# A two-layer hybrid encoder: residual tiles in other buffers, and weight-splitting subtractions on GpSimd

## The chip, the cores and the metric

One core of a Trainium2 chip runs the kernel. The metric is the device time in microseconds (us) of one execution. The kernel before took 1229.7 us (median of 3 runs, 1227.62 to 1229.96).

## The reference

Two layers act on 512 tokens of width 1024, in float32. Each layer has a mixing half and an MLP half:

```
h = rmsnorm(x) @ w_in                       # split into parts for A, B and C
o_a = dilated biased attention   (6 heads)  # softmax(q k + bias) v
o_b = windowed biased attention  (4 query heads on 2 key heads, a sink logit)
o_c = latent attention, no bias  (6 heads, low-rank q and kv, rotary part)
mixed = concat(rmsnorm(o_a), rmsnorm(o_b), rmsnorm(o_c))
x = x + mixed @ w_out
x = x + relu(rmsnorm(x) @ w_up)^2 @ w_down
```

C is the "unbiased" attention, A and B are the biased ones.

## The kernel before, in words

**Number format.** Every matmul with float32 operands is made of products of a hi and a lo part. `split` (line 362) makes hi by a copy into the reduced format (ScalarE or VectorE, whichever the planner thinks is done first) and lo by a subtraction, source minus hi, on VectorE. `mm3` (line 403) adds three products: hi by hi, hi by lo, lo by hi. Weights go through `wload` (line 387): a DMA into one of two "raw" buffers, then `wsplit` (line 393) into one of four "whi" and four "wlo" buffers (NW, line 27).

**Order of the work.** The program text records operations; nothing is emitted until `Plan.schedule` (line 207) has put all of them in one order. It is a list scheduler: again and again it takes the operation that can start earliest by its estimated costs (`Plan.cost`, line 146), and among equals the one that stands first in the text. Buffers with one tag are handed out in the order of the text, apart from PSUM banks, which go in any order. Each engine, and the queue of DMA issues on SyncE, then runs its part of that order strictly in sequence. So text order sets priorities and buffer order, and an operation from further down fills gaps if its inputs and buffers are free.

**The mixing half** (`mix`, line 532). The input projections are cut into eight column groups, win0 and win(1) to win(7), of four 576-column or two 1024-column weight tiles each. The steps after the latent preparation are named in one string (line 911): w3 to w7 are input projections, C0 to C2 two heads each of the latent attention, A0 to A2 two heads each of the dilated attention, B0 and B1 two heads each of the windowed attention, gC and gA the group norms. Group B's norm follows (line 919). Then the residual x is loaded: `x_tiles` (line 341) puts three of its four 128-token blocks into the tile "v", which until then holds the values of attention A, and the fourth into a "ma" buffer, which attention A and B use for their bias rows (`master`, line 822). Line 925 issues the four loads. The output projection follows (lines 928 to 940), one group of w_out tiles after the other: C (3 tiles), A (3 tiles), B (2 tiles). For each half of the columns and each token block, a bank sums the products of the group, and VectorE adds the bank, scaled by the group's rstd, to the residual (line 936). After group B's add come the sums of squares and `norm_in` (line 447), the transposed input of the MLP.

The query and key tiles of attention C (`qc`, `kc`, line 644) are the two "tm9" buffers; the rotary and bias setup uses them before that (`setup`, line 463), with four loads and one store on GpSimd's queue.

**The MLP half** (`mlp`, line 956) works in four chunks. `pieces` (line 945) takes its hidden tiles from buffers that the mixing half no longer needs: "tm12", both "tm9" and one "ma" for the larger ones.

Of the kernel before, what the change touches and what calls it, by code (L numbers as in the profile page):

```python
# [10 lines left out]
F32 = mybir.dt.float32  # L11
F32R = mybir.dt.float32r
I32 = mybir.dt.int32
AF = mybir.ActivationFunctionType
OP = mybir.AluOpType
AX = mybir.AxisListType

D = 1024
# [3 lines left out]
NB = S // 128  # L22
# [3 lines left out]
FM = 16  # L26
NW = 4
QK = 4

G1, G2, GO, GQL, GKL, GQA, GKA, GQB, GKB, GQC, GKC, GQR, GKR, SNK, NPAR = (  # L30
    0, 8, 16, 24, 26, 27, 28, 29, 30, 31, 32, 33, 65, 97, 101)
# [90 lines left out]
class Plan:  # L122
# [23 lines left out]
    def cost(self, eng, method, out, ins):  # L146
        if method == "dma_start" and eng == "gpsimd":
            return 1000.0
        n = max([out.size() if isinstance(out, View) else 0] + [v.size() for v in ins if method == "tensor_reduce"])
        psum = any(v.buf.psum for v in ins) or (isinstance(out, View) and out.buf.psum)  # L150
        if eng == "tensor":
            if ins[0].dtype == F32R:
                return n / 2.4 + 12.5
            f = 2.0 if method == "transpose" else 4.0
            return f * max(n / 2.4, 54.0) + 2.0
        if eng == "vector":
            fast = method in ("tensor_scalar", "tensor_copy") and not psum and n > 64
            side = 60.0 if method in ("tensor_scalar", "scalar_tensor_tensor") and any(
                v.size() == 1 for v in ins[1:]) or method == "tensor_tensor_reduce" else 0.0
            return 70.0 + side + n / (1.92 if fast else 0.96) * (8.0 if method == "reciprocal" else 1.0)  # L160
        if eng == "scalar":
            return 93.0 * (len(ins) - 1) + (55.0 if psum else 95.0) + n / 1.2
        return 50.0 + n * 4 * 128 / 340.0

    def either(self, *calls):
# [5 lines left out]
    def record(self, eng, method, args, kw, alt=None):  # L171
# [6 lines left out]
        if alt:  # L178
            alt.alts[eng] = (method, args, kw, cost)
            return  # L180
        o = Op()
        o.i, o.alts = len(self.ops), {eng: (method, args, kw, cost)}
        o.after, o.need, o.bufs = set(), {self.gate} if self.gate else set(), []
        for views, write in ((ins, False), (outs, True)):
# [114 lines left out]
def kernel(  # L299
# [12 lines left out]
    pe, dve, act, dma, gps = (plan.engine(e) for e in ("tensor", "vector", "scalar", "sync", "gpsimd"))  # L312

    def T(shape, dtype, tag, bufs=1, pool="sb"):
        return plan.tile(pool, shape, dtype, tag, tag, bufs)

    def bank():
        return T([128, 512], F32, "bank", 8, "psum")

    def fmt(dt=F32R):  # L320
        return T([128, 512], dt, "fm", FM)

    def f32(a):
        return a.bitcast(F32)
# [14 lines left out]
    xs = T([S, D], F32, "xs", 1, "dram")  # L339

    def x_tiles():

        a, b = T([128, 3072], F32, "v", 1), T([128, 1024], F32, "ma", 2)
        return [a[:, i * D:(i + 1) * D] for i in range(3)] + [b[:, :D]]

    con_sb = T([128, 272], F32, "con_sb", 1)
    gps.dma_start(con_sb[:], con)
# [1 line left out]

    def P(l, i, n=1):  # L350
        return par_sb[:, l * NPAR + i:l * NPAR + i + n]


    def copy(out, src, scale=None):

        if scale is None:
            plan.either(("scalar", "activation", (out, src, AF.Copy), {}), ("vector", "tensor_copy", (out, src), {}))
        else:
            plan.either(("scalar", "activation", (out, src, AF.Copy), {"scale": scale}),
                        ("vector", "tensor_scalar", (out, src, scale, None, OP.mult), {}))  # L360

    def split(hi, lo, src, scale=None):

        copy(hi, src, scale)
        if scale is None:
            dve.tensor_tensor(lo, src, f32(hi), OP.subtract)
        else:
            dve.scalar_tensor_tensor(lo, src, scale, f32(hi), OP.mult, OP.subtract)
# [18 lines left out]
    def wload(src):  # L387
        n = src.shape[1]
        raw = T([128, 1024], F32, "raw", 2)[:, :n]
        dma.dma_start(raw, src)  # L390
        return wsplit(raw)

    def wsplit(raw):
        n = raw.a.shape[1]
        hi = T([128, 1024], F32R, "whi", NW)[:, :n]
        lo = T([128, 1024], F32R, "wlo", NW)[:, :n]
        split(hi, lo, raw)
        return hi, lo

    def at(w, c):  # L400
        return w[0][:, c], w[1][:, c]

    def mm3(out, a, b, start, stop):

        pe.matmul(out, a[0], b[0], start=start, stop=False, skip_group_check=True)
        pe.matmul(out, a[0], b[1], start=False, stop=False, skip_group_check=True)
        return pe.matmul(out, a[1], b[0], start=False, stop=stop, skip_group_check=True)
# [39 lines left out]
    def norm_in(k, gain):  # L447

        pt = bank()
        for b in range(NB):  # L450
            pe.transpose(pt[:, b * 128:(b + 1) * 128], x_t[b][:, k * 128:(k + 1) * 128], ident)
        hi, lo = fmt(), fmt()
        split(hi[:], lo[:], pt[:], gain)
        return hi, lo
# [77 lines left out]
    def mix(l, xg, st1):  # L532
# [48 lines left out]
        def qk4():  # L581
            g = T([128, 4, S], F32R, "qk", QK)
            return [g[:, i] for i in range(4)]
# [10 lines left out]
        vb = T([128, NB, 2, 3, 64], F32R, "vb", 1)  # L594
# [19 lines left out]
        for t in range(3):  # L614
# [3 lines left out]
            hi, lo = q4[2 * t:2 * t + 2]  # L618
# [224 lines left out]
        def group(os, first, mul, name):  # L843
            st = Stat(len(os), mul, name)
            for o in os:
                st.add(o)
            r = st.rstd()
            for i, o in enumerate(os):
                hi, lo = fmt(), fmt()
                split(hi[:], lo[:], o, P(l, GO + first + i))  # L850
                og[first + i] = (hi, lo)
            return r

        def ot(n):
            g = T([128, 3, S], F32, "o", 2)
            return [g[:, i] for i in range(n)]

        o_c, o_a = ot(3), ot(3)
# [35 lines left out]
        o_b = ot(2)  # L894
# [13 lines left out]
                       lambda qb: (max(0, qb - 1), min(NB - 1, qb + 1)), ls)  # L908
            normalise(o_b[pr], ls, rev)

        for step in "w3 C0 C1 C2 w4 w5 gC A0 A1 w6 A2 w7 gA B0 B1".split():
            if step == "gC":
                rc = group(o_c, 5, 1.0 / 384, "grc")
            elif step == "gA":
                ra = group(o_a, 0, 1.0 / 384, "gra")
            else:
                {"C": step_c, "w": step_w, "A": step_a, "B": step_b}[step[0]](int(step[1]))

        rb = group(o_b, 3, 1.0 / 256, "grb")


        nonlocal x_t
        x_t = x_tiles()
        for b in range(NB):
            dma.dma_start(x_t[b], (x if l == 0 else xs)[b * 128:(b + 1) * 128, :])
        st2 = Tokens("r2")
        xg2 = []
        for n, (ts, r) in enumerate((((5, 6, 7), rc), ((0, 1, 2), ra), ((3, 4), rb))):
            w = [wload(w_out[l, :, t * D:(t + 1) * D]) for t in ts]
            for h in range(2):  # L930
                hs = slice(h * 512, h * 512 + 512)
                for b in range(NB):
                    ps = bank()
                    for i, t in enumerate(ts):
                        mm3(ps[:], at(og[t], slice(b * 128, (b + 1) * 128)), at(w[i], hs), i == 0, i == len(ts) - 1)
                    dve.scalar_tensor_tensor(x_t[b][:, hs], ps[:], r[:, b:b + 1], x_t[b][:, hs], OP.mult, OP.add)
                    if n == 2:
                        st2.add(b, h)
                if n == 2:
                    xg2 += [norm_in(k, P(l, G2 + k)) for k in range(4 * h, 4 * h + 4)]  # L940
        return xg2, st2


# [1 line left out]
    def pieces():  # L945

        big, small = [], []
        for to, n, tag, w, bufs, k in ((big, 1024, "tm12", 3072, 1, 1), (big, 1024, "tm9", 2304, 2, 2),
                                       (big, 1024, "ma", 1024, 2, 1), (small, 768, "vb", 1536, 1, 1),
                                       (small, 768, "tm6", 1664, 1, 1), (small, 768, "o", 1536, 2, 2)):  # L950
            for _ in range(k):
                t = T([128, w], F32R, tag, bufs)
                to += [t[:, i * n:(i + 1) * n] for i in range(w // n)]
        return [(small[2 * j], small[2 * j + 1], big[2 * j], big[2 * j + 1]) for j in range(4)]

    def mlp(l, xg2, st2):
# [12 lines left out]
        for c in range(CH):  # L969
            quarter = []  # L970
            for q in range(4):
                t = T([128, 2048], F32, "qk", QK)
                dma.dma_start(t[:], w_down[l, :, (c * 4 + q) * 2048:(c * 4 + q + 1) * 2048])
# [83 lines left out]
    x_t = None  # L1057
    st1 = Stat(KT, 1.0 / D, "r1")
    xg = []
    for l in range(DEPTH):  # L1060
        xg2, st2 = mix(l, xg, st1)
        xg, st1 = mlp(l, xg2, st2)
    plan.emit()

# [90 lines left out]
```

## Time and profile before

| | before |
|---|---|
| median of 3 runs | 1229.7 us |
| profiled execution | 1230.45 us |
| its span, first to last instruction | 1228.7 us |
| mean granted TensorE clock | 0.993 |
| TensorE matmuls busy | 1203.5 us |
| VectorE busy | 1014.5 us |
| ScalarE busy | 629.0 us |
| GpSimd busy | 3.5 us |

The first layer's mixing half ends at about 273 us of the span; its MLP half reaches to about 631 us, where the second layer repeats the pattern. In the rows, PE is TensorE, PEld its weight loads, DVE VectorE, ACT ScalarE, POOL GpSimd, SP SyncE; "q" marks an engine's queue that issues DMAs. Nearly all operations carry line 295, where the planner emits them, so they are told apart by their tiles, written out<-in. Tiles "tm" are those of the tags tm6, tm9 and tm12. Matmul ends are modelled, so the distance of two starts tells more of TensorE's pace than a matmul's length.

### The profile page before, as it was taken

To read this page: it belongs to the slowest core of one execution; us is meant where nothing else is said; L and a number is where in the kernel's file an instruction comes from. 1 tells how busy PE (TensorE), PEld (TensorE's weight loads), DVE (VectorE), ACT (ScalarE), POOL (GpSimd) and SP (SyncE) were. 2 spreads that over 40 slices of the span, in tenths; PEclk is the share of its full clock that TensorE was granted. 3 is DMA by queue.
4 is the path that set the end of the run, shared out by engine and by line. 5 is a ranking of instruction groups with operands and counts; after the bars stand their busy time and mean duration, and the time that the engine had idled before them with its cause. 6 is when DMAs were issued, how large, how long until landed. Compare 5 with 4: busy or idle time off the path is not lost.

```text
span 1228.7 us, 17782 instructions
## 1 busy us (share of the span) xinstructions
PE 1203.5 (98%) x6624; PEld 1032.6 (84%) x6624; DVE 1014.5 (83%) x1907; ACT 629.0 (51%) x1232; POOL 3.5 (0%) x10
## 2 busy tenths in 40 slices
PE   9999999899999999999999999898999999999998
PEld 8998979788888888888899989786888888888886
DVE  7799879798796886977958996997978869779686
ACT  6658678455343333333546684965544334334342
POOL 1000000000000000000000000000000000000000
PEclk9999999899999999999999999998999999999999
DMA  6311254533133042140152114454331422422301
GB/s 197 125 52 53 50 147 132 150 137 121 68 122 118 35 173 102 71 135 20 53 166 72 50 52 102 136 146 136 131 117 38 165 79 79 155 71 103 103 1 69
DMA packets 36357, 123.89 MB, mean 101 GB/s; under 512 B 4700, under 2 KB 5852, under 8 KB 32176
## 3 DMA queue, kind: packets, MB, share of 16 engines
q1 hardware_dynamic: 36048, 122.41, 31.7%
q8 instruction: 52, 0.85, 0.3%
q0 software_dynamic: 224, 0.36, 0.1%
q14 instruction: 33, 0.27, 0.1%
HBM read 108.29 MB, written 4.24 MB: 92 GB/s over the span
## 4 chain that ended last, share of the span: by engine, by line
PE 85%; ACT 7%; DVE 4%; DMA 2%; issue 2%; SPq 0%; ACTq 0%; DVEq 0%
PE bank L295 85%; ACT p L295 3%; ACT pt L295 2%; DVE p L295 1%; DVE pt L295 1%; ACT pvt L295 1%; ACT sq L295 1%; DVE wlo L295 1%; DMA v<-in_xT_dram 0%; DMA qk<-qk 0%; DVE v L295 0%; ACT tm L295 0%; DMA v<-in_x_dram 0%; DVE o L295 0%; ACT fm L295 0%
## 5 line engine op out<-in xcount | busy, mean ns | idle before, releaser
L295 PE MATMUL bank<-fm,whi 128*128 128x512 f32 x1024 | 315.8, 390 | 0.0
L295 PE MATMUL bank<-whi,fm 128*128 128x256 f32 (+2 forms) x1280 | 288.2, 310 | 1.3 <-ACT whi L295 1.0
L295 PEld LDWEIGHTS bank<-fm,whi 128*128 128x128 f32 x1024 | 192.2, 188 | 39.9
L295 PEld LDWEIGHTS bank<-whi,fm 128*128 128x128 f32 x1280 | 211.5, 190 | 13.0 <-ACT whi L295 1.3
L295 ACT ACTIVATE whi<-raw 128x1024 fp32r<-128x1024 f32 (+2 forms) x110 | 112.3, 1023 | 209.0 <-PE bank L295 157.1
L295 DVE TENSOR_TENSOR wlo<-raw,whi 128x1024 fp32r<-128x1024 f32 (+2 forms) x122 | 142.4, 1169 | 79.3 <-ACT whi L295 78.9
L295 PE MATMUL bank<-fm,wlo 128*128 128x512 f32 x512 | 199.3, 390 | 0.0
L295 PE MATMUL bank<-wlo,fm 128*128 128x256 f32 (+2 forms) x640 | 197.3, 309 | 0.2 <-DVE wlo L295 0.2
L295 PE MATMUL bank<-whi,tm 128*128 128x512 f32 x544 | 177.2, 390 | 0.0
L295 PEld LDWEIGHTS bank<-wlo,fm 128*128 128x128 f32 x640 | 121.6, 190 | 6.4 <-DVE fm L295 0.9
L295 ACT ACTIVATE whi<-pt 128x1024 fp32r<-128x1024 f32 x64 | 68.0, 1063 | 109.6 <-PE bank L295 90.1
L295 PEld LDWEIGHTS bank<-whi,tm 128*128 128x128 f32 x544 | 102.1, 188 | 22.2
L295 PE MATMUL bank<-wlo,tm 128*128 128x512 f32 x304 | 118.7, 390 | 0.0
L295 PEld LDWEIGHTS bank<-fm,wlo 128*128 128x128 f32 x512 | 96.1, 188 | 19.9
L295 ACT ACTIVATE whi<-qk 128x1024 fp32r<-128x1024 f32 x48 | 50.9, 1059 | 100.7 <-PE bank L295 100.7
L295 PE MATMUL bank<-qk 96*128 96x512 f32 (+3 forms) x304 | 89.8, 401 | 5.6 <-issue 4.5
L295 DVE TENSOR_TENSOR wlo<-qk,whi 128x1024 fp32r<-128x1024 f32 x48 | 57.9, 1219 | 31.0 <-ACT whi L295 31.0
L295 DVE TENSOR_TENSOR pt<-bank,pt 128x512 fp32r<-128x512 f32 (+2 forms) x128 | 79.4, 633 | 4.1 <-ACT pt L295 2.3
L295 PE MATMUL bank<-con_sb,p 128*128 128x128 f32 x464 | 75.9, 285 | 5.8 <-DVE nm L295 1.7
L295 DVE TENSOR_TENSOR wlo<-pt,whi 128x1024 fp32r<-128x1024 f32 x64 | 77.9, 1217 | 1.2 <-ACT whi L295 1.2
L295 ACT ACTIVATE pt<-bank 128x512 fp32r<-128x512 f32 (+2 forms) x128 | 68.7, 555 | 3.3 <-PE bank L295 2.0
L295 ACT ACTIVATE p<-p,nm 128x512 f32<-128x512 f32 (+2 forms) x80 | 52.0, 651 | 33.6 <-DVE nm L295 33.5
(182 smaller groups left out, 1867.6 us busy)
## 6 DMA issues: line engine op xcount, KB each, us to landing
qk<-in_w_down_dram SPq DMA_DIRECT2D x32, 1024.0 KB, 4.6
raw<-in_w_up_dram SPq DMA_DIRECT2D x64, 512.0 KB, 3.3
raw<-in_w_in_dram SPq DMA_DIRECT2D x28, 512.0 KB, 3.4
qk<-qk SPq DMA_DIRECT2D x78, 128.0 KB, 2.4
raw<-in_w_out_dram SPq DMA_DIRECT2D x16, 512.0 KB, 3.8
ma<-brow SPq DMA_DIRECT2D x12, 448.0 KB, 4.0
raw<-in_w_in_dram SPq DMA_DIRECT2D x8, 288.0 KB, 3.6
v<-in_xT_dram SPq DMA_DIRECT2D x6, 256.0 KB, 6.2
```

What stands on the lines that cost most here:

```text
L295: getattr(getattr(nc, o.eng), o.name)(*[real(a) for a in o.args], **{k: real(v) for k, v in o.kw.items()})
```

## The change

The residual is loaded right after group C's norm (step x) into the two "tm9" buffers, two blocks in each. The output projections become steps of the order string: pC and pA stand before gB, pB last. In the mixing halves `wsplit` makes hi on ScalarE always and lo on GpSimd; the planner gets a cost for GpSimd. The MLP's larger hidden tiles come from "tm12", "v" and both "ma" buffers.

```diff
+ORDER = "w3 C0 C1 C2 w4 w5 gC x A0 A1 w6 A2 w7 gA B0 B1 pC pA gB pB"
...
+        if eng == "gpsimd":
+            return 100.0 + 2.3 * n
...
     def x_tiles():
-        a, b = T([128, 3072], F32, "v", 1), T([128, 1024], F32, "ma", 2)
-        return [a[:, i * D:(i + 1) * D] for i in range(3)] + [b[:, :D]]
+        return [t[:, i * D:(i + 1) * D] for t in (T([128, 2304], F32, "tm9", 2), T([128, 2304], F32, "tm9", 2)) for i in range(2)]
...
+    mixing = [False]
...
         lo = T([128, 1024], F32R, "wlo", NW)[:, :n]
-        split(hi, lo, raw)
+        if mixing[0]:
+            act.activation(hi, raw, AF.Copy)
+            gps.tensor_tensor(lo, raw, f32(hi), OP.subtract)
+        else:
+            split(hi, lo, raw)
         return hi, lo
...
-        for step in "w3 C0 C1 C2 w4 w5 gC A0 A1 w6 A2 w7 gA B0 B1".split():
...
-        rb = group(o_b, 3, 1.0 / 256, "grb")
...
-        x_t = x_tiles()
-        for b in range(NB):
-            dma.dma_start(x_t[b], (x if l == 0 else xs)[b * 128:(b + 1) * 128, :])
-        st2 = Tokens("r2")
-        xg2 = []
-        for n, (ts, r) in enumerate((((5, 6, 7), rc), ((0, 1, 2), ra), ((3, 4), rb))):
+        def project(ts, r, done):
             w = [wload(w_out[l, :, t * D:(t + 1) * D]) for t in ts]
...
-                    if n == 2:
+                    if done:
                         st2.add(b, h)
...
+        st2 = Tokens("r2")
+        xg2, r = [], {}
+        for step in ORDER.split():
+            n = int(step[1]) if step[1:].isdigit() else step[1:]
+            if step == "x":
+                x_t = x_tiles()
+                for b in range(NB):
+                    dma.dma_start(x_t[b], (x if l == 0 else xs)[b * 128:(b + 1) * 128, :])
+            elif step[0] == "g":
+                o, t, m = {"C": (o_c, 5, 384), "A": (o_a, 0, 384), "B": (o_b, 3, 256)}[n]
+                r[n] = group(o, t, 1.0 / m, "gr" + n.lower())
+            elif step[0] == "p":
+                project({"C": (5, 6, 7), "A": (0, 1, 2), "B": (3, 4)}[n], r[n], n == "B")
+            else:
+                {"C": step_c, "w": step_w, "A": step_a, "B": step_b}[step[0]](n)
...
-        for to, n, tag, w, bufs, k in ((big, 1024, "tm12", 3072, 1, 1), (big, 1024, "tm9", 2304, 2, 2),
-                                       (big, 1024, "ma", 1024, 2, 1), (small, 768, "vb", 1536, 1, 1),
+        for to, n, tag, w, bufs, k in ((big, 1024, "tm12", 3072, 1, 1), (big, 1024, "v", 3072, 1, 1),
+                                       (big, 1024, "ma", 1024, 2, 2), (small, 768, "vb", 1536, 1, 1),
...
+        mixing[0] = True
         xg2, st2 = mix(l, xg, st1)
+        mixing[0] = False
         xg, st1 = mlp(l, xg2, st2)
```

## Rows read from the trace of the kernel before

**Rows 1.** Engines of the page: busy us, share of the span, instructions
```profile
PE 1203.5 (98%) x6624; PEld 1032.6 (84%) x6624; DVE 1014.5 (83%) x1907; ACT 629.0 (51%) x1232; POOL 3.5 (0%) x10
```

**Rows 2.** Busy time by stage: us, PE PEld DVE ACT POOL, clock, DMA share, GB/s
```profile
75.00:125.00 50.00, 48.26 (x342) 43.16 (x341) 48.17 (x100) 41.87 (x95) 0.00 (x0) 1.00 0.14 43
125.00:150.00 25.00, 24.96 (x204) 24.46 (x204) 21.78 (x61) 15.76 (x37) 0.00 (x0) 1.00 0.13 32
150.00:212.00 62.00, 58.93 (x426) 52.68 (x425) 52.46 (x133) 47.92 (x116) 0.00 (x0) 1.00 0.54 141
229.80:247.90 18.10, 14.35 (x76) 11.18 (x75) 13.85 (x49) 13.24 (x45) 0.00 (x0) 0.81 0.26 94
247.90:273.00 25.10, 25.10 (x134) 20.60 (x134) 24.67 (x56) 14.74 (x38) 0.00 (x0) 1.00 0.48 168
836.20:854.30 18.10, 14.37 (x68) 11.12 (x67) 13.02 (x46) 12.52 (x42) 0.00 (x0) 0.72 0.27 93
```

**Rows 3.** Groups of TensorE in 229.8 to 247.9 us: busy us, mean ns
```profile
L295 PE MATMUL bank<-con_sb,p 128*128 128x128 f32 x25 | 6.0, 359 | 1.3 <-ACT p L295 0.7 <-DVE nm L295 0.6
L295 PE MATMUL bank<-pt,vb 128*128 128x256 f32 x16 | 4.1, 355 | 0.2 <-DVE pt L295 0.2
L295 PE MATMUL bank<-qk 128*128 128x384 f32 x12 | 4.0, 402 | 0.1
```

**Rows 4.** Timeline of TensorE where it is dense: start us, length us
```profile
286.06 0.60 PE L295 MATMUL bank<-con_sb,v 128*128 128x128 f32 x4
286.41 0.48 PE L295 MATMUL bank<-fm,wlo 128*128 128x512 f32 x1
...
294.68 0.39 PE L295 MATMUL bank<-fm,wlo 128*128 128x512 f32 x1
...
295.36 0.39 PE L295 MATMUL bank<-fm,wlo 128*128 128x512 f32 x1
```

**Rows 5.** Waits by engine: us in total, times, longest us
```profile
DVE v L295 <- DMA v<-xs: 4.2, 1, 4.2
```

**Rows 6.** Timeline of VectorE, 224 to 234 us
```profile
227.37 0.15 DVE L295 SCALAR_TENSOR_TENSOR gra<-rs_b,rs_y 128x4 f32<-128x4 f32 x1
231.08 1.41 DVE L295 SCALAR_TENSOR_TENSOR v<-bank,grc,v 128x512 f32<-128x512 f32 x2 [3.56 <-DMA v<-in_x_dram]
```

**Rows 7.** Timeline of the queue of DMA issues, first layer
```profile
38.45 77.23 SPq L295 DMA_DIRECT2D raw<-in_w_in_dram  x10
140.68 0.33 SPq L295 DMA_DIRECT2D raw<-in_w_out_dram  x1
...
247.02 0.33 SPq L295 DMA_DIRECT2D ma<-in_x_dram  x1
```

**Rows 8.** Timeline of TensorE, the last transposes of attention C's queries and keys
```profile
121.72 0.60 PE L295 MATMUL bank<-con_sb,tm 128*96 128x128 f32 x4
```

**Rows 9.** The tile in_x_dram: its loads, issue to landing
```profile
DMA to landing us min/median/max: 3.5/4.6/5.4
```

**Rows 10.** Timeline of TensorE, 256 to 266 us: the sums over group B's heads
```profile
264.88 1.05 PE L295 MATMUL bank<-one,ssum 128*128 128x1 f32 x8
```

**Rows 11.** Groups of the first mixing half, 0 to 273 us: busy us, mean ns
```profile
L295 DVE TENSOR_TENSOR wlo<-raw,whi 128x1024 fp32r<-128x1024 f32 x21 | 25.4, 1214 | 1.8 <-ACT whi L295 1.7
...
L295 ACT ACTIVATE whi<-raw 128x1024 fp32r<-128x1024 f32 x19 | 20.0, 1060 | 23.4 <-DMA raw<-in_w_in_dram 12.2 <-PE bank L295 11.1
...
L295 DVE CAST whi<-raw 128x1024 fp32r<-128x1024 f32 x4 | 2.7, 685 | 1.0 <-PE bank L295 1.0
```

**Rows 12.** Timelines of TensorE and GpSimd: start us, length us, idle before and its end
```profile
15.51 1.02 PE L295 MATMUL bank<-tm,tm 32*10 32x512 f32 x2
...
26.06 0.52 POOL L295 DMA_DIRECT2D brow<-tm  x1 [21.99 <-DVE rs_a L295]
```

**Rows 13.** Groups of VectorE, 0 to 273 us
```profile
L295 DVE TENSOR_TENSOR ssum<-ssum,sq 128x512 f32<-128x512 f32 x12 | 8.2, 684 | 0.0
```

More of the change, by code (lines that the diff above doesn't have):

```diff
@@ L909, in step_b @@
             normalise(o_b[pr], ls, rev)
-        for step in "w3 C0 C1 C2 w4 w5 gC A0 A1 w6 A2 w7 gA B0 B1".split():
[L912 to L917, printed above, removed]
-        rb = group(o_b, 3, 1.0 / 256, "grb")
-        nonlocal x_t
-        x_t = x_tiles()
-        for b in range(NB):
-            dma.dma_start(x_t[b], (x if l == 0 else xs)[b * 128:(b + 1) * 128, :])
-        st2 = Tokens("r2")
-        xg2 = []
-        for n, (ts, r) in enumerate((((5, 6, 7), rc), ((0, 1, 2), ra), ((3, 4), rb))):
+        def project(ts, r, done):
             w = [wload(w_out[l, :, t * D:(t + 1) * D]) for t in ts]
@@ L936, in mix @@
                     dve.scalar_tensor_tensor(x_t[b][:, hs], ps[:], r[:, b:b + 1], x_t[b][:, hs], OP.mult, OP.add)
-                    if n == 2:
+                    if done:
                         st2.add(b, h)
-                if n == 2:
-                    xg2 += [norm_in(k, P(l, G2 + k)) for k in range(4 * h, 4 * h + 4)]
+                if done:
+                    xg2.extend(norm_in(k, P(l, G2 + k)) for k in range(4 * h, 4 * h + 4))
+        nonlocal x_t
+        st2 = Tokens("r2")
[13 more added lines that the diff above has]
+                {"C": step_c, "w": step_w, "A": step_a, "B": step_b}[step[0]](n)
         return xg2, st2
```

## The prediction

> **What bounds the kernel now.** I read the page's engine table first [rows 1]: TensorE is busy for 98% of the span, so a faster VectorE is worth only what TensorE waits for it. The stage table [rows 2] shows where TensorE is not fed. In 75 to 125 us (latent attention) and 150 to 212 us (biased attention) it lacks 1.7 and 3.1 us, with VectorE busy for 48.2 of 50 and 52.5 of 62 us. GpSimd does nothing in any of these rows. The poor stretch is 229.8 to 247.9 us, with its repeat in the second layer at 836.2: TensorE shows 14.4 us busy out of 18.1, at a granted clock of 0.81 and 0.72, a mean over parts at 2.4 and parts at 1.2 GHz. Right after, 247.9 to 273, it is full again at clock 1.00.
>
> What work was in the poor stretch? The groups of TensorE there [rows 3] are transposes, scores and PV products of the grouped-query attention (step B) and nearly no projection. In dense stretches [rows 4] three 512-column matmuls start in 0.68 us (0.227 each) and four transposes in 0.35 us (0.088 each); by columns I estimate 0.17 for 384 and 0.114 for 256. So the stretch holds 25 x 0.088 + 16 x 0.114 + 12 x 0.17 = 6.1 us, and the other 23 of its 76 instructions, priced as 256 columns, 2.6: some 8.6 us of work in 18.1 us, **9.5 us lost**. The second layer's stretch has the same length, fewer instructions (68) and a lower clock, so it loses no less: 19 us for both.
>
> Why? The waits [rows 5] show VectorE held by the residual's loads for 4.2 us in the second layer, and its timeline in the first [rows 6] shows what that does: adds of projection C stand in front of step B's first score and hold VectorE from 227.4 to 231.1 us. The last load is issued only at 247.0 us [rows 7], because its buffer, "ma", still serves step B's biases. Until then that block's banks are not evicted, projection C's weight tiles stay held, and projection A, which has no other obstacle, can't start.
>
> **The change, part by part.**
>
> *Residual in "tm9" from step x.* The last transposes that read the query and key tiles there start at 121.7 us [rows 8]. The queue of DMA issues then has nothing between 115.7 (38.45 + 77.23) and 140.7 us [rows 7], and DMA is 13% busy in 125 to 150 [rows 2]. Four loads a layer, landing after 3.5 to 5.4 us [rows 9], fit there: I cost the moved issues at nothing. The cover is that gap; they go ahead of the w_out loads, the qk copies and the bias loads of 140 us and later, and if the planner set them among those, a copy could wait for one load, up to 5 us once a layer. They leave the stretch in which step B's own copies run.
>
> *Projections C and A inside step B.* Projection A alone is 8 banks x 9 matmuls x 0.227 = 16.3 us of work, more than the 9.5 us lost. What sets the end then is projection B, which needs group B, whose sum over heads comes at 264.9 us now [rows 10]. The work done up to 273 us, without the loss, would end near 263.5; step B's chain loses the wait of 3.6 us on VectorE but shares VectorE with A's adds (0.7 us each, as C's in rows 6). I leave 1 us a layer lost in front of projection B: 19 - 2 = **17.0 us gained**. The bounds are nothing (the chain slips by as much) and 19.
>
> *lo parts on GpSimd.* By the code there are 29 subtractions a layer: 22 of 1024 columns, 6 of 576, 1 of 768. VectorE spends 1.21 us on one of 1024 [rows 11], by columns some 0.7 and 0.9 on the others: 26.6 + 4.2 + 0.9, about 32 us a layer, go. No row shows GpSimd computing on a whole tile. From below I bound its price by VectorE's 1.21 us; from above by the pace at which weights are used: a 1024-column tile of the input projections feeds 48 matmuls of 256 columns, 48 x 0.114 = 5.5 us, and beyond that GpSimd would be the bound. I take twice VectorE's time, 2.4 us, nearer to the row. Throughput is then covered, and four buffers of each part let tiles be ready ahead. Where they aren't (the first tile, the changeover from projection C to A) lo comes 0.7 to 1.2 us later, partly hidden by the products of the hi parts: +1.5 us in all, between 0 and 5. The Trainium skill (GPSIMD Engine Reference, Performance versus the Vector engine) states 4497 ns for 2048 columns, by which I would estimate some 2.3 us; nothing in the sum hangs on that.
>
> What VectorE gets back is worth at most TensorE's idle time in the two attention stretches, 1.7 + 3.1 us a layer [rows 2]. With a tenth to a fifth of VectorE's work gone I take back 3 us of the 9.6, between 0 and 8.
>
> *hi parts on ScalarE alone.* VectorE made 4 of the wide ones in the first layer, at 0.69 us; ScalarE takes 1.06 us for one [rows 11]. Some 4 us more a layer, on an engine with 9 us free in the 25 of 125 to 150 us [rows 2]: nothing. Without that cover it would be those 4 us.
>
> *GpSimd's own queue.* The setup loads are issued by 4.1 us now (26.06 less an idle time of 21.99), ahead of TensorE's setup product at 15.5 us [rows 12]. Behind the first or second subtraction they go out 5 to 10 us later, and TensorE's queue, which is in order, waits for them: 0 to 5 us once; I take +1.5. Behind the store of the bias row, which waits for VectorE until 26.1 us, one or two subtractions could queue, and the products that read them; those tiles are asked for ahead: nothing.
>
> *MLP pieces in "v" and "ma", group B after A in the text.* "v" is last read by step A, "ma" by step B's biases, both before the MLP writes them; TensorE loses nothing in 247.9 to 273 now. The order of the groups in their buffers stays C, A, B. Nothing.
>
> Sum: -17.0 - 3 + 1.5 + 1.5 = -17.0 us. The profiled execution took 1230.45 us (its span 1228.7 and 1.75 around it), 0.75 above the median of 1229.7; so **1213.5 us**. A measurement of this kernel can tell some 0.2%, 2.5 us, from no change.
>
> **A rule that speaks against it.** In these rows GpSimd never computes beside VectorE, so none shows whether they hinder each other. The Trainium skill (SBUF — State Buffer, Who interferes with whom) says that a VectorE instruction with two SBUF inputs and a GpSimd instruction that reads SBUF exclude one another: the second waits for the end of the first. By it the 3 us of relief become none, 1216.5 us, and more where the wait falls into a chain; no run here shows it yet, and it stands below as a rival, priced from rows.
>
> **The rivals.**
> - *Exclusion (the slower side).* VectorE's sums of squares add two SBUF tiles [rows 13], and its normalising and rstd chains do the like; with 133 instructions in 62 us [rows 2], about five of all kinds fall into a subtraction of 2.4 us, so most subtractions would hold VectorE once, for half their length, 1.2 us. If half of the 58 fall into a chain that TensorE waits for, 29 x 1.2 = 35 us are lost: 1230.45 - 17 + 35 = 1248. It decides from 17 / 58 = 0.3 us per subtraction that reach TensorE. For it: VectorE's load in 75 to 125 us. Against: attention's own instructions read a bank and at most one SBUF tile, and TensorE has other work in most stretches.
> - *Step B stays the bound.* A's eight adds (8 x 0.7, near 6 us) delay its chain, so some of TensorE's idle time moves in front of projection B: 4 us a layer, gain 17 - 8 = 9, 1221.5. For it: VectorE and ScalarE each already work 13 to 14 of the 18 us in which TensorE starves [rows 2]. Against: 3.6 us of the chain go.
> - *Full relief.* VectorE's 32 us a layer free 8 us of the attention stretches' idle time and step B leaves nothing: 1230.45 - 19 - 8 + 1.5 = 1205. Against: the same load on ScalarE, 41.9 of 50 us [rows 2].
> - *It doesn't do what it says*: the planner issues the loads late again. Nothing reads "tm9" after 121.7 us, so I give it no chance of its own.
>
> **How the numbers follow.** Forecast 0.52 (its own range 1208 to 1220), step B as the bound 0.15, full relief 0.13, exclusion 0.20. Of the last I put 0.06 within 0.2% (gain and loss cancel) and 0.14 above. Faster 0.80, same 0.06, slower 0.14. The range runs from 1202, full relief with its other terms at their best, to 1230, where exclusion has eaten the gain; left out are some 0.15 above and a little below.
>
> **What would show it.** Right: the residual's loads issued at 120 to 140 us and no wait of VectorE for them; projection A's 512-column matmuls between 230 and 250 us, at clock 1.00; mixing halves some 8 us shorter each, MLP halves unchanged; GpSimd near 2.4 us a tile. Wrong: VectorE's two-input instructions held beside GpSimd, TensorE waiting for "wlo", a gap in front of projection B or behind the setup loads at 10 to 20 us.

## The result, and the profile after

The changed kernel took **1303.9 us** (median of 4 runs, 1300.77 to 1305.47) against 1229.8 for the kernel before on the same chip: a ratio of 1.060, 95% interval 1.0589 to 1.0615, 74 us slower. The forecast was 1213.5 within 1202 to 1230, so both the sign and the range were wrong. The profiled execution took 1304.59 us, its span 1302.8, at a mean granted clock of 0.971 (0.993 before). From these means I estimate that TensorE stood at 1.2 GHz, the lower of its two levels, for some 76 us, 17 before. The lower clock is part of the loss, and no run here separates it from the rest.

The engines on the page of the kernel after, beside [rows 1]:

```profile
PE 1234.9 (95%) x6624; PEld 1052.4 (81%) x6624; DVE 1032.2 (79%) x1861; ACT 631.1 (48%) x1220; POOL 137.7 (11%) x68
```

Some 64 us of subtractions left VectorE, and yet its busy time rose from 1014.5 to 1032.2 us. So its other instructions took some 82 us more, and no table of waits shows why. By stage (columns as in [rows 2]):

```profile
0.00:75.00 75.00, 60.95 (x408) 57.31 (x409) 52.24 (x137) 40.19 (x97) 29.17 (x23) 0.92 0.42 130
75.00:125.00 50.00, 43.76 (x252) 38.13 (x252) 47.72 (x127) 31.92 (x72) 14.89 (x4) 0.81 0.14 46
150.00:212.00 62.00, 57.33 (x435) 52.75 (x434) 42.07 (x105) 37.52 (x91) 14.43 (x6) 1.00 0.42 112
250.00:275.00 25.00, 20.16 (x90) 15.86 (x89) 16.03 (x59) 8.72 (x27) 0.00 (x0) 0.79 0.29 81
320.00:610.00 290.00, 290.00 (x1284) 238.86 (x1283) 231.72 (x284) 112.08 (x138) 0.00 (x0) 1.00 0.29 99
675.00:725.00 50.00, 43.91 (x335) 42.97 (x335) 33.61 (x88) 24.39 (x72) 16.85 (x8) 0.97 0.24 70
```

The MLP (320 to 610 us) is full as it was. The time went in the mixing halves. Much of it went before 125 us, in the first input projections (0 to 75 us: 408 matmuls started) and in the latent attention's preparation (75 to 125 us: 252 started, 342 before, at a mean granted clock of 0.81). The kernel before, from 0 to 75 us:

```profile
0.00:75.00 75.00, 71.67 (x529) 68.23 (x530) 60.54 (x201) 47.70 (x120) 3.53 (x10) 1.00 0.47 146
```

Step B's poor stretch is still there, now around 250 to 275 us, at 0.79.

What does a held instruction look like? VectorE's timeline of the kernel after, in the first layer (start us, length us):

```profile
63.87 0.18 DVE L298 SCALAR_TENSOR_TENSOR rs_a<-rs_i 128x16 f32<-128x16 f32 x1
64.08 2.38 DVE L298 TENSOR_TENSOR rs_b<-rs_a,rs_v 128x16 f32<-128x16 f32 x1
66.38 0.44 DVE L298 TENSOR_REDUCE ssq<-sq 128x3 f32<-128x288 f32 x1
```

and GpSimd's timeline of the same kernel, with one subtraction that starts 0.05 us before it and one later:

```profile
64.03 2.40 POOL L298 TENSOR_TENSOR wlo<-raw,whi 128x1024 fp32r<-128x1024 f32 x1 [13.11 <-ACT whi L298]
...
90.53 7.23 POOL L298 TENSOR_TENSOR wlo<-raw,whi 128x1024 fp32r<-128x1024 f32 x1 [2.74 <-ACT whi L298]
```

A multiplication of 16 columns, 0.17 us elsewhere, lasts 2.38 us and ends with GpSimd's instruction (64.03 + 2.40). At 90.53 it goes the other way round: VectorE runs normalising and rotary instructions back to back, and GpSimd's 2.4 us become 7.23. All rs_b instructions of the kernel before and then of the kernel after (groups by tile: ns min/median/max):

```profile
L295 DVE TENSOR_TENSOR rs_b<-rs_a,rs_v x78: 147/165/183, 25.0 to 904.4; 128x4 f32<-128x4 f32 x30, 128x16 f32<-128x16 f32 x24, 128x8 f32<-128x8 f32 x12, 128x24 f32<-128x24 f32 x12
```

```profile
L298 DVE TENSOR_TENSOR rs_b<-rs_a,rs_v x78: 142/166/2386, 30.5 to 977.5; 128x4 f32<-128x4 f32 x30, 128x16 f32<-128x16 f32 x24, 128x8 f32<-128x8 f32 x12, 128x24 f32<-128x24 f32 x12
```

The median has not moved; single instructions are 2.2 us longer. I summed these over the trace: an instruction of VectorE counts as held if it overlaps GpSimd's work on a tile and is over 0.1 us longer than the median of the same instruction in the kernel before (those without a counterpart there are left out). That gives 38 held instructions and 63 us, most of the 82. Of these, 22 instructions and 42 us belong to rstd chains (some ten small instructions each that make one over a root mean square; their tiles are rs_...). What TensorE sees of two of them, in the timelines of VectorE and then of TensorE:

```profile
47.93 1.25 DVE L298 SCALAR_TENSOR_TENSOR rs_y<-rs_b,rs_i 128x8 f32<-128x8 f32 x1
49.22 1.72 DVE L298 SCALAR_TENSOR_TENSOR rs_a<-rs_y 128x8 f32<-128x8 f32 x1
```

```profile
44.32 0.28 PE L298 MATMUL bank<-wlo,fm 128*128 128x256 f32 x1
52.40 0.90 PE L298 MATMUL bank<-con_sb,tm 128*128 128x128 f32 x3 [7.79 <-DVE tm L298]
```

Both belong to the rstd chain behind which "tm" is scaled. They add 2.6 us to that chain. The other 5 us of TensorE's wait are the rest of the chain and what stands in front of it. In the kernel before TensorE had work for that time (it is busy for 24.3 of the 25 us from 25 to 50 us), here it had none left. So what a hold costs also hangs on what covers its chain.

### The profile page after: what moved, and what is told of

Read it like the earlier page. It is cut to its first block, busy times and chain, and to the rows that moved or that the text cites. A ratio compares the mean times of both kernels' runs of the same rounds, so it can differ in the third digit from the quotient of the medians.

```text
span 1302.8 us, 17854 instructions
## 1 busy us (share of the span) xinstructions
PE 1234.9 (95%) x6624; PEld 1052.4 (81%) x6624; DVE 1032.2 (79%) x1861; ACT 631.1 (48%) x1220; POOL 137.7 (11%) x68
## 5 line engine op out<-in xcount | busy, mean ns | idle before, releaser
L298 PE MATMUL bank<-whi,fm 128*128 128x256 f32 (+2 forms) x1280 | 293.3, 317 | 5.8 <-ACT sq L298 4.9
L298 PEld LDWEIGHTS bank<-whi,fm 128*128 128x128 f32 x1280 | 218.4, 197 | 18.0 <-ACT sq L298 5.6
L298 POOL TENSOR_TENSOR wlo<-raw,whi 128x1024 fp32r<-128x1024 f32 (+2 forms) x58 | 134.2, 2317 | 811.4 <-ACT whi L298 806.5
L298 ACT ACTIVATE whi<-raw 128x1024 fp32r<-128x1024 f32 (+2 forms) x118 | 120.5, 1022 | 204.0 <-PE bank L298 122.5
L298 PE MATMUL bank<-wlo,fm 128*128 128x256 f32 (+2 forms) x640 | 203.5, 318 | 1.6 <-POOL wlo L298 1.6
L298 PEld LDWEIGHTS bank<-wlo,fm 128*128 128x128 f32 x640 | 126.2, 197 | 8.1 <-POOL wlo L298 2.1
L298 DVE TENSOR_TENSOR wlo<-raw,whi 128x1024 fp32r<-128x1024 f32 x64 | 81.3, 1271 | 64.1 <-ACT whi L298 63.8
L298 PE MATMUL bank<-whi,tm 128*128 128x512 f32 x288 | 98.5, 392 | 0.0
L298 PEld LDWEIGHTS bank<-con_sb,p 128*128 128x128 f32 x464 | 55.4, 148 | 21.5 <-ACT pt L298 4.6
L298 PE MATMUL bank<-con_sb,tm 128*128 128x128 f32 (+1 forms) x288 | 47.1, 305 | 26.2 <-DVE tm L298 25.4
```

The source lines that it names most:

```text
L298: getattr(getattr(nc, o.eng), o.name)(*[real(a) for a in o.args], **{k: real(v) for k, v in o.kw.items()})
```

## The experiments

Each run was timed in three rounds against the kernel before, which gave 1229.2 to 1229.7 us as the median beside them.

### The order alone, and GpSimd alone

The changed kernel with the weight tiles split as before:

```diff
-        if mixing[0]:
-            act.activation(hi, raw, AF.Copy)
-            gps.tensor_tensor(lo, raw, f32(hi), OP.subtract)
-        else:
-            split(hi, lo, raw)
+        split(hi, lo, raw)
```

> The changed kernel with hi and lo of the weight tiles made as before (lo on VectorE): the residual's buffers, the order of the projections and the MLP's buffers are left alone. Theory 1 (GpSimd's subtractions and VectorE's instructions hold each other): the whole loss of 74 us comes with the subtractions, so this kernel falls below the kernel before, 1215 to 1228 us; it does not reach 1213, since in the changed kernel the banks and weight buffers still kept projection A out of step B. Theory 2 (the new order costs the time: projections C and A take banks and VectorE from step B): 1245 us or more. Theory 3 (the loss is made in equal parts by both): near 1265.

Measured: 1235.3 us, ratio 1.0045 (1.0029 to 1.0062). This is none of the three theories' numbers: the order costs 6 us instead of gaining, and some 69 us come with the way the weight tiles are split, that is GpSimd's subtractions together with hi on ScalarE.

The kernel before with lo of the mixing halves alone on GpSimd (the flag and the planner's cost for GpSimd are as in the changed kernel):

```diff
-        split(hi, lo, raw)
+        if mixing[0]:
+            copy(hi, raw)
+            gps.tensor_tensor(lo, raw, f32(hi), OP.subtract)
+        else:
+            split(hi, lo, raw)
```

> The kernel before with only lo of the mixing halves' weight tiles on GpSimd; hi, the residual's buffers and the order string as before. Theory 1 (mutual holding): 1285 to 1310 us, with VectorE instructions of 16 or 24 columns that last 2 us and more beside a subtraction. Theory 2 (order): within 10 us of the kernel before.

Measured: 1294.9 us, ratio 1.0536 (1.0514 to 1.0559): GpSimd's subtractions cost 66 us in the old order too, with 35 held instructions and 55 us.

### Is it lo's lateness, or the holding?

Here VectorE makes lo as before, and GpSimd then works on the raw tile, which nobody reads any more. Two kernels in the same planned order differ in one instruction:

```diff
         split(hi, lo, raw)
+        if mixing[0]:
+            gps.tensor_tensor(raw, raw, f32(hi), OP.subtract)   # run 1
+            gps.memset(raw, 0.0)                                # run 2
```

> The kernel before, VectorE makes lo as before, and GpSimd makes the same subtraction a second time, into the raw tile that nobody reads any more. So lo is never late for a product; only raw is held longer. Theory 1 (holding): 30 to 70 us above the kernel before, since the price is VectorE's waiting and not lo's lateness. Theory 4 (lateness: GpSimd's 2.4 us in place of 1.2 us delay the products): within 10 us of the kernel before.

> As the run with the subtraction made twice, in the same planned order, but GpSimd fills the dead raw tile with zeros in place of the subtraction, so it reads nothing from SBUF. Theory 1 in the form that GpSimd's reading of SBUF is what excludes VectorE: within 8 us of the kernel before, small VectorE instructions beside a fill keep their 0.2 us. Theory 5 (any GpSimd instruction on SBUF holds VectorE, or the later release of raw costs the time): as far above the kernel before as the run with the subtraction, in proportion to GpSimd's busy time.

Measured: **1281.5 us** with the subtraction, ratio 1.042 (1.040 to 1.044), and **1232.7 us** with the fill, ratio 1.0029 (1.002 to 1.0039). GpSimd's groups and timeline, and VectorE's timeline, in the run with the subtraction:

```profile
L297 POOL TENSOR_TENSOR raw<-raw,whi 128x1024 f32<-128x1024 f32 x44 | 107.0, 2433 | 431.3 <-DVE wlo L297 264.4 <-issue 36.9 <-ACT pt L297 30.3
...
80.77 5.68 POOL L297 TENSOR_TENSOR raw<-raw,whi 128x1024 f32<-128x1024 f32 x2 [7.78 <-DVE rs_y L297]
...
81.69 2.42 DVE L297 SCALAR_TENSOR_TENSOR rs_a<-rs_y 128x24 f32<-128x24 f32 x1
84.03 0.21 DVE L297 TENSOR_TENSOR tbk<-sn,par_sb 128x64 f32<-128x64 f32 x1
84.17 2.33 DVE L297 TENSOR_TENSOR rs_b<-rs_a,rs_v 128x24 f32<-128x24 f32 x1
```

The same views in the run with the fill:

```profile
L297 POOL MEMSET raw<- 128x1024 f32 x44 | 42.5, 965 | 450.7 <-DVE wlo L297 292.0 <-ACT pt L297 26.7 <-DVE rqa L297 23.8
...
66.80 0.95 POOL L297 MEMSET raw<- 128x1024 f32 x1 [0.18 <-DVE rs_a L297]
...
66.71 0.21 DVE L297 TENSOR_TENSOR tbk<-sn,par_sb 128x64 f32<-128x64 f32 x1
66.84 0.17 DVE L297 TENSOR_TENSOR rs_b<-rs_a,rs_v 128x24 f32<-128x24 f32 x1
66.96 0.85 DVE L297 TENSOR_SCALAR tbk<-tbk 128x64 f32<-128x64 f32 x1
```

lo is made on VectorE in both, so GpSimd's lateness is no part of the 49 us between them. With the subtraction 31 instructions of VectorE are held for 50 us; the time is 52 us above the kernel before. With the fill, multiplications of two tiles run beside it at their usual 0.17 to 0.21 us; only a TENSOR_SCALAR waits for its end (66.96 + 0.85 is 67.81, the fill ends at 67.75).

The same count by kind of instruction tells which are held. Beside the subtraction they are 26 of 42 with two operands in SBUF and 5 of 9 TENSOR_SCALARs with one, but none of the 95 that read a bank and none of 22 TENSOR_REDUCEs. Beside the fill they are 6 of 7 TENSOR_SCALARs from SBUF and 3 of 59 instructions with two operands there.

Two other causes could lie in the 49 us. The raw buffer is free later behind the subtraction than behind the fill (2.4 us against 1.0). But by the tables of waits TensorE and its weight loads together wait for weight parts for 8.7 us with the subtraction and 3.2 with the fill, so at most 5.5 us lie there. And the mean granted clock is 0.979 against 0.994; the lower clock comes with the starving and is in the 49 us.

Does a hold last to the end of GpSimd's instruction? The next kernel cuts each repeated subtraction into four:

```diff
-            gps.tensor_tensor(raw, raw, f32(hi), OP.subtract)
+            for i in range(4):
+                q = slice(i * n // 4, (i + 1) * n // 4)
+                gps.tensor_tensor(raw[:, q], raw[:, q], f32(hi)[:, q], OP.subtract)
```

> As the run in which GpSimd repeats the subtraction into the dead raw tile (1281.5 us, 52 over the kernel before), but each repeat is cut into four instructions of a quarter of the columns; GpSimd's work and its operands are the same. Theory 1 in the form that an instruction is held until the other engine's current instruction ends: one hold lasts at most 0.6 us instead of 2.4, and the loss falls to 13 to 25 us, 1242 to 1255. Rival (the two engines share the bandwidth of one port, so that only the columns moved count): the loss stays near 52 us, 1275 to 1290.

Measured: 1271.3 us, ratio 1.034 (1.0324 to 1.0355). Timelines of GpSimd and VectorE:

```profile
83.48 4.32 POOL L297 TENSOR_TENSOR raw<-raw,whi 128x256 f32<-128x256 f32 x6
...
85.01 0.74 DVE L297 SCALAR_TENSOR_TENSOR rs_a<-rs_y 128x24 f32<-128x24 f32 x1
85.67 1.47 DVE L297 TENSOR_TENSOR rs_b<-rs_a,rs_v 128x24 f32<-128x24 f32 x2
87.06 0.78 DVE L297 SCALAR_TENSOR_TENSOR rs_y<-rs_b,rs_i 128x24 f32<-128x24 f32 x1
```

A single hold is now some 0.6 us, as a hold to the end of the instruction gives, but the saving I expected from it did not come: a chain meets the next quarter with its next instruction, so 76 instructions are held instead of 31, for 34 us in place of 50. The loss fell from 52 to 42 us only. GpSimd, for its part, is busy for longer (183 us in place of 130).

### Where on the path do the holds cost most?

The first kernel splits the tiles of w_in's groups 0 to 2, w_uq and w_ukv as before and uses GpSimd from step w3 on (the flag is set ahead of the order's loop):

```diff
+        mixing[0] = True
         for step in ORDER.split():
```

> The changed kernel (1304 us) with hi and lo as before up to step w3 (input column groups 0 to 2, w_uq, w_ukv: lo on VectorE), and on GpSimd from w3 on. Theory 1 (holding, dear where VectorE runs chains of small instructions on SBUF tiles: rstd, rotary parts, sums of squares): the first 75 us of each layer win back most of what they lost, 1255 to 1275 us, the rest stays with w3 to w5 beside the rotary part. Rival (late lo or the setup loads behind the subtractions at the start are the main price): the setup alone is once, under 5 us, so 1300.

Measured: 1286.2 us, ratio 1.046 (1.0445 to 1.0476), 18 us less than the changed kernel and not the 30 to 50 expected. Its first 50 us are as before (TensorE busy for 46.6), but the first subtraction now starts at 53.5 us and meets the rstd and rotary chains all the same; 28 instructions stay held for 49 us.

The second uses GpSimd for w_out's eight tiles a layer alone, in the better order of the next section:

```diff
+            mixing[0] = True
             w = [wload(w_out[l, :, t * D:(t + 1) * D]) for t in ts]
+            mixing[0] = False
```

> The kernel with the new order and the held scores, and of the weight tiles only w_out's eight a layer with hi on ScalarE and lo on GpSimd. There VectorE mostly reads banks, which GpSimd's subtraction did not hold. Theory 1 with that reading: within 4 us of the same kernel without GpSimd, either way. Relief theory (VectorE is short of time in step B): 3 to 8 us faster than it. Holding in all places: 29 of 58 holds, 10 us or more slower.

Measured: 1223.6 us, ratio 0.9953 (0.9938 to 0.9968), 12 us slower than the same kernel without it (1211.6), and not within 4 us as expected. Only 10 instructions are held, for 12.2 us, although the attention beside it mostly reads banks. That the two numbers agree is in part chance: TensorE also waits for "wlo" for 3.1 us in this run, and hi is on ScalarE. One of the ten, with one operand, in the timelines of GpSimd and then of VectorE:

```profile
215.04 2.41 POOL L298 TENSOR_TENSOR wlo<-raw,whi 128x1024 fp32r<-128x1024 f32 x1 [15.30 <-ACT whi L298]
```

```profile
215.47 2.01 DVE L298 TENSOR_SCALAR rs_v<-ssqa 128x16 f32<-128x16 f32 x1
```

### Why did step B stay starved?

In the run with the order alone the residual is loaded long before and VectorE waits for no load, yet TensorE is busy for 14.7 us of 20.2 only, at a granted clock of 0.75 (stage table of that run):

```profile
232.40:252.60 20.20, 14.71 (x71) 11.31 (x71) 15.18 (x50) 14.86 (x47) 0.00 (x0) 0.75 0.49 147
```

In the changed kernel's timeline of TensorE, step B's scores come in bursts of eight matmuls, two to a bank:

```profile
262.48 1.34 PE L298 MATMUL bank<-qk 128*128 128x256 f32 x8
263.66 0.40 PE L298 MATMUL bank<-wlo,fm 128*128 128x512 f32 x1
263.90 0.39 PE L298 MATMUL bank<-whi,fm 128*128 128x512 f32 x1
264.13 1.53 PE L298 MATMUL bank<-qk 128*128 128x256 f32 x8
```

These two bursts take eight banks, as many as the kernel has. Scores need only the query and key tiles and stand ahead of the projections in the text, so the planner can give them every bank that comes free. Projection C's seventh add comes at 264.3 us, its eighth at 289.8, and until then its three weight tiles stay held. The test is to let the planner set a score of step B only behind the eviction of the second score before it:

```diff
+                    if ahead and len(seen) >= ahead:      # 2 in step B, 0 elsewhere
+                        plan.gate = seen[-ahead]
                     score(qb, sc, j0, nk)
+                    plan.gate = None
...
+                    if ahead:
+                        seen.append(<the eviction just recorded>)
```

> The kernel with the new order and lo on VectorE (1235 us), and one thing more: in the planner's order a score of step B may stand only behind the eviction of the second score before it; nothing else changes. Theory 6 (step B's scores run ahead, each takes a bank, and so the planner places projection A behind step B): projection A's 512-column matmuls now lie between step B's, the two poor stretches of some 9.5 us go, 1210 to 1222 us. Rival 7 (step B's own chain on ScalarE and VectorE sets the end, or the weight splits that stand in front of its softmax there): no change within 5 us, or slower, as scores come later.

Measured, with lo on VectorE: **1211.6 us**, ratio 0.9859 (0.9842 to 0.9875), below both kernels. TensorE's groups in 225 to 250 us, first of the run with the order alone, then of this one, with this one's stage:

```profile
L298 PE MATMUL bank<-whi,fm 128*128 128x512 f32 x15 | 4.9, 391 | 0.0
```

```profile
225.00:250.00 25.00, 25.00 (x151) 21.73 (x150) 22.99 (x68) 17.81 (x57) 0.00 (x0) 1.00 0.53 154
...
L298 PE MATMUL bank<-whi,fm 128*128 128x512 f32 x41 | 14.2, 402 | 0.0
```

The projections now lie between step B's instructions, 41 of their hi matmuls in place of 15, and the clock stays at 1.00. Did the residual's place matter at all? The same hold in the kernel before:

> The kernel before with the held scores alone: a score of step B may be planned only behind the eviction of the second score before it. The residual is still loaded at the end into the tiles of attention A and a bias buffer. The prediction's cause (the residual's late loads hold VectorE and projection C's banks, so A can't start): the poor stretch stays, 1225 us or more. Theory 6 (the scores take the banks, whatever the residual does): the poor stretch goes here too, 1211 to 1220 us; the move of the residual is then worth the difference to the run with both, 1211.6.

Measured: 1215.2 us, ratio 0.9885 (0.987 to 0.9899). Its stage and its queue of DMA issues:

```profile
225.00:250.00 25.00, 23.85 (x143) 20.06 (x142) 22.67 (x72) 18.27 (x56) 0.00 (x0) 1.00 0.65 177
...
246.19 0.33 SPq L295 DMA_DIRECT2D ma<-in_x_dram  x1
```

The last block is issued at 246.2 us, as late as in [rows 7], and the poor stretch is gone all the same. So the scores that run ahead were the cause; that they do it through the banks is argued from the bursts above. The new order (the residual, the projections and the MLP's buffers together) is worth 3.6 us beside the hold (1215.2 to 1211.6), which is hardly clear of the noise, since the intervals of the two ratios just overlap. Without the hold it cost 6.

### The other parts, in the order with held scores

> The changed kernel (1304 us) with the held scores alone. If the banks of step B and the holding by GpSimd are two costs that add, it gains the 24 us that the same hold gave with lo on VectorE: 1275 to 1285 us. If GpSimd's holding sets step B's pace anyway, 1295 or more.

> The new order with held scores, lo on VectorE, and hi of the mixing halves' weight tiles on ScalarE always, as in the changed kernel. The prediction's term (ScalarE has the time, nothing): within 3 us of 1211.6. Rival (hi stands in ScalarE's queue ahead of attention's exponentials and waits there for a weight buffer): 4 us a layer, near 1219.

> As the run with hi on ScalarE always, but the lo parts of the mixing halves' weight tiles are left out: GpSimd fills them with zeros behind hi, which held VectorE for 4 us in all in the run with fills, and VectorE loses 32 us of work a layer. The planner is given the fill's measured 0.9 us. What it tells is what VectorE's relief is worth without the holding. The prediction's term: 3 us faster than with lo on VectorE (0 to 8), 1204 to 1212. Rival 8 (with VectorE relieved the planner sets the input projections earlier, and TensorE has nothing left beside the latent attention's normalising chain): slower than it, 1215 to 1225.

The edits are the hold in the changed kernel, and, in place of GpSimd's subtraction there, one on VectorE (`dve.tensor_tensor`), or a fill that leaves lo out (`gps.memset(f32(lo), 0.0)`, planned behind hi). Each row changes one thing more:

| kernel | us | ratio (interval) | step |
|---|---|---|---|
| new order, held scores | 1211.6 | 0.9859 (0.9842 to 0.9875) | |
| hi on ScalarE always | 1215.8 | 0.9889 (0.9874 to 0.9903) | +4.2 |
| lo a fill on GpSimd: VectorE relieved | 1225.3 | 0.9964 (0.9951 to 0.9977) | +9.5 |
| lo subtracted on GpSimd | 1281.4 | 1.0423 (1.0406 to 1.0441) | +56.1 |
| scores not held: the changed kernel | 1303.9 | 1.0602 (1.0589 to 1.0615) | +22.5 |

The first step is hardly clear of the noise either (the two intervals touch). Rows 2 and 4 differ by one edit, lo on VectorE or on GpSimd: 65.6 us, with 38 held instructions and 63 us of holds.

The third row surprises. The stages of the run with hi on ScalarE, and then of the run with the fill:

```profile
60.00:80.00 20.00, 20.00 (x166) 20.00 (x166) 20.00 (x74) 10.44 (x23) 0.00 (x0) 1.00 0.26 80
80.00:100.00 20.00, 19.13 (x134) 17.03 (x133) 18.65 (x46) 16.98 (x38) 0.00 (x0) 1.00 0.10 27
```

```profile
60.00:80.00 20.00, 18.06 (x134) 15.87 (x132) 20.00 (x78) 13.48 (x27) 1.91 (x2) 1.00 0.36 106
80.00:100.00 20.00, 18.78 (x111) 15.88 (x112) 18.87 (x45) 16.82 (x41) 0.00 (x0) 0.91 0.00 1
```

In 60 to 100 us TensorE starts 245 matmuls instead of 300, while VectorE, busy for nearly all of it in both, works on the latent attention's normalising chain. What is missing there are products with weight tiles. TensorE's matmuls that read "whi" (us, busy, clock, DMA share, GB/s), in the run with hi on ScalarE and then in the run with the fill:

```profile
60.00:100.00 40.00, 25.53 (x133) 1.00 0.18 53
...
120.00:140.00 20.00, 4.07 (x20) 1.00 0.13 48
```

```profile
60.00:100.00 40.00, 10.23 (x57) 0.96 0.18 54
...
120.00:140.00 20.00, 15.22 (x80) 1.00 0.13 31
```

Up to 60 us the second run is ahead by only 14 of them (249 to 235); most of what covered the chain now comes after it. So the planner set the cover elsewhere. This run also gives the planner a shorter time for GpSimd, so the 9.5 us are the relief together with another plan, and which of the two moved the projections stays open. The step of 56.1 us takes in lo's lateness; the pair of runs with lo on VectorE puts the holding at 49.

## Why the prediction was wrong

**The larger failed step: lo on GpSimd, put at +1.5 us of lateness and -3 us of relief.** The sum had no term for VectorE's instructions being held; the holding stood beside it as a rival at 0.20. The runs showed some 69 us for the split on GpSimd and ScalarE (1235.3 to 1303.9), most of it holding: 49 us by the pair of runs with lo on VectorE. That is about three quarters of the 90 us between forecast and measurement; the order is the rest.

**The other failed step: "projection A, which has no other obstacle, can't start".** It took the residual's wait of 3.6 us on VectorE for the cause of the 9.5 us lost. It was no more than a symptom: with the residual as late as before and the scores held, TensorE is busy for 23.85 us of 25 at a clock of 1.00. The obstacle was step B's scores, planned ahead, with the banks that they take and projection C's weight tiles behind them. In place of -17.0 the order gave +6. The mechanism behind the gain (projections as cover for step B) was sound: with the scores held it is worth 14 us in the kernel before and 18 in the new order.

**The rival that should have been the forecast: exclusion, 0.20 at 1248 us.** Its mechanism is what happened. The Trainium skill (SBUF — State Buffer, Who interferes with whom) states it, and also that GpSimd instructions that only write don't hinder a VectorE instruction with two SBUF inputs; the traces agree with both (2.38 us beside a subtraction, 0.17 beside a fill). Of the 56 us between 1248 and the measured time, 23 are the order (+6 in place of -17), which the rival shared; the rest is its price. What failed were the two halves of its price. "Held for half their length, 1.2 us" was too little: 38 holds make 63 us, 1.65 us each. "Half fall into a chain that TensorE waits for" was too little as well: the time lost is about the sum of the holds in every run, or above it (52 against 50 us with lo on VectorE, 12.0 against 12.2 with w_out alone, 66 against 55 in the old order, 42 against 34 with the quarters), with the lower clock and lost cover in it. And "attention's own instructions read a bank" overlooked what stands in line with them: group norms, rstd chains and lsum sums, ahead of evictions on the same engine.

**Relief of VectorE, -3 (0 to -8).** Wrong in sign as far as it was tried: +9.5 in the fill run, together with the other plan that it got.

**hi on ScalarE, nothing.** +4.2 us in all, hardly clear of the noise. Its cover was 9 us free in one stage, and where hi costs the time stays open.

**What held.** The price of one subtraction, 2.4 us: the one at 64.03 takes 2.40, and the mean of the 44 of that size is 2.56 with the 7.23 among them. lo's lateness: TensorE waited for "wlo" for 1.6 us in the whole run and its weight loads for 2.1, within 0 to 5. The residual's loads, issued in the gap, with no wait for them (queue of DMA issues in the kernel after):

```profile
136.14 4.32 SPq L298 DMA_DIRECT2D tm<-in_x_dram  x4
```

The MLP halves are unchanged. The setup loads do go out behind subtractions, the last at 19.4 us, but the first setup product starts at 16.0 us in place of 15.5 [rows 12], without a wait of TensorE in front of it. So that term, +1.5, was nearly nothing:

```profile
16.03 1.02 PE L298 MATMUL bank<-tm,tm 32*10 32x512 f32 x2
```

**The bounds.** Neither large error had room in its bounds: the order's gain was put between nothing and 19, with no room for a loss, and the exclusion had one price, a mean hold, outside the sum.

## What to carry to other kernels

Moving element work from VectorE to GpSimd was priced here by the instructions of VectorE that ran beside it with two operands in SBUF (or a TENSOR_SCALAR from SBUF), each of which could wait for a whole GpSimd instruction, and not by GpSimd's own time; a VectorE busy time that doesn't fall when work leaves it is the sign. If an engine starves although work is ready, look at who holds the banks and buffers which that work needs before blaming the wait that the profile names; one limit on how far a producer runs ahead gained 14 us in the kernel before and 24 in the new order. And relief of an engine that isn't the bound can come out slower, when the planner's order changes with it and a chain loses its cover.

## What was unexpected of the hardware

- Holding runs both ways, and to the end of an instruction: 0.17 us became 2.38 on VectorE; under an unbroken run of VectorE's SBUF instructions 2.4 us became 7.23 on GpSimd.
- Cutting GpSimd's instruction into four shortened a hold to 0.6 us but raised the number from 31 to 76, so the sum fell by a third only (50 to 34 us).
- A fill on GpSimd takes 0.97 us for 1024 columns, a subtraction 2.43, and beside a fill an instruction with two SBUF inputs runs at its full pace while a TENSOR_SCALAR with one waited 0.65 us for its end; beside a subtraction one took 2.01 us in place of 0.17.
